# A hybrid decoder block: recurrent output transposed a step sooner and in pairs, weight casts placed behind the bank copies at every border, and the operand differences of one feed-forward block placed behind low parts

## The chip, the cores and the metric

The kernel runs on one core of a Trainium2 chip. The metric is the device time of one execution in microseconds (us); lower is better. Three runs of the kernel before are given, and one more execution was recorded by the profiler; all durations of single instructions come from that recording.

A core has a matrix engine (PE, with its weight loader PEld), a vector engine (DVE), an activation engine (ACT), a general engine (POOL) and an engine that here only issues transfers (SP). Each runs its own instructions in its own order, and they wait for one another by semaphores.

## The reference

One decoder layer over 512 positions of width 2048, in float32. Its input projection feeds eight attention heads and eight heads of a gated linear recurrence; their outputs are joined for one output projection, and a squared-ReLU network follows.

```python
h = rms_norm(x, norm1_w) * (1 + scale1) + shift1
aq, ak, av, gq, gf, gi, gg = split(h @ w_in)              # 2048 x 7168
attn = rms_norm(dilated_attention(norm_rope(aq), norm_rope(ak), av))
hg = rms_norm(hgrn2(gq, gf, gi, lb)) * silu(gg)           # 8 heads of 128
x = x + gate1 * (concat(attn, hg) @ w_out)                # 2048 x 2048
h2 = rms_norm(x, norm2_w) * (1 + scale2) + shift2
x = x + gate2 * (square(relu(h2 @ w_ff1)) @ w_ff2)        # 2048 x 8192, 8192 x 2048
```

`shift`, `scale` and `gate` are six rows that a matrix-vector product makes from the condition `c`.

## The kernel before

**Number format.** Every large product is made of three matmuls of a reduced float32 format: both operands are split into a high part (a cast on ACT) and a low part (source minus high part, on DVE). For weights this is `_split` (the cast is L39, the subtraction L40), for the activations `split_to` (L246 and L247). A matmul reads a 128x128 stationary tile and a 128x512 moving one and adds to one of eight banks; three matmuls (L205 to L207) belong to each pair of tiles.

**Input projection.** `project` (L375) computes 512 output columns in 16 steps of k, 128 rows of the weight each, with twelve matmuls a step into four banks of the tag `mm`. Its weights come in pairs of steps through `load_w` (L191): one transfer, two casts, two subtractions, with four buffers each. After the last step the four banks are copied out on ACT (`evac` L414, `hgrn_q` L572, `hg_gate` L716), and the next projection writes the same four banks; this place is called a border below. `load_w` can place its two casts behind a bank copy (`cast_behind`, used for the second pair of a projection, `k0 == 2`): the copy is kept in the list `evacuated`, which in this version only `hg_gate` fills. So the placement acts at two borders, ahead of the second gate projection and ahead of the output projection.

**Background work.** Attention, recurrence and output steps are generators in the list `tasks`; `tick` runs one step of the first of them after each step of k, so the code between two `yield`s lands between two steps of a projection. PE keeps exactly the order in which the code issues its instructions (a manual schedule from the first value projection on). ACT, DVE, POOL and SP are ordered by a scheduler ahead of the run, by priority and estimated readiness; `tc.issue_after(x)` forces an instruction to stand behind x, and `high_priority` lets it stand earlier.

**Recurrent output.** `hg_out` (L725) normalises each head's output and multiplies it by its gate (four DVE instructions of 128x128 a head, L731), and in the next step `to_mix` (L552) transposes it with four matmuls against the identity (L555) and copies the result on ACT into a tile `mix` (L557). `split_mix` splits that tile (L246, L247) into the left operand of the output projection. `korder` puts the four recurrent heads of the first group first, then eight attention heads, then the second recurrent group. The gate projection of the second group (`hg_gate(1)`) is the last ahead of the output projection, `project_out(0)`, whose first steps therefore need heads 0 to 3 of the first recurrent group, one a step. There two ticks follow each of the first ten steps.

**Feed-forward.** Both products use a seven-product scheme: per block of 1024 columns, seven products (order 1, 5, 6, 7, 3, 4, 2) of 48 matmuls (L1200 to L1202), each with four weight tiles of 128x1024. Products 5, 6, 7 and 4 need a difference of two weight tiles, made on DVE in place (`sum_of`, L1168), then the cast (L1184, ACT) and the low part (L1185, DVE). In the first feed-forward product each difference is tied behind a recent low part (`tie`); in the second product (stage 2, blocks (q, c)) it is not, and the scheduler may place several in a row.

Of the kernel before, what the change touches and what calls it, by code (L numbers as in the profile page):

```python
# [22 lines left out]
DH = 128  # L23
# [21 lines left out]
def hybrid_block(ctx, tc, x, c, positions, norm1_w, w_ada, b_ada, w_in, q_norm_w, k_norm_w,  # L45
# [3 lines left out]
    pe, dve, act, pool = nc.tensor, nc.vector, nc.scalar, nc.gpsimd  # L49
# [18 lines left out]
    def bank(name, tag="bg"):  # L68
        return ps.tile([P, 512], F32, name=name, tag=tag)
# [30 lines left out]
    n2c, aoc, hgc, posc = cols[:, 0:16], cols[:, 16:24], cols[:, 40:41], cols[:, 44:48]  # L100
# [88 lines left out]
    evacuated = []  # L189
# [45 lines left out]
    def slot(name, dt=F32):  # L235
        return io.tile([P, 512], dt, name=name, tag="io")
# [44 lines left out]
    for q in range(4):  # L281
# [5 lines left out]
        for j in range(4):  # L287
# [3 lines left out]
            t = slot("xnT")  # L291
# [117 lines left out]
    def evac(banks, name):  # L409
        ts = []  # L410
        for ti in range(NT):
            t = slot(name)
            with tc.high_priority():
                act.copy(t, banks[ti])  # L414
            ts.append(t)
        return ts

# [134 lines left out]
    def to_mix(k, src, hs, wcol):  # L552
        pt = bank("ptm")
        for ti in range(NT):
            pe.transpose(pt[:, ti * P:(ti + 1) * P], src[ti][:, hs], ident)  # L555
        mix[k] = slot("mix")
        act.activation(mix[k], pt, AF.Identity, scale=wcol)  # L557
# [8 lines left out]
    def hgrn_q(ht):  # L566
        qb = project(3072 + ht * 512, ch_mm)
        qs = []
        for h in range(4):
            q = slot("gq")  # L570
            with tc.high_priority():
                act.copy(q, qb[h])  # L572
            qs.append(q)
        for q in qs:
            sg = wk.tile([P, 512], F32, name="sg", tag="ev", bufs=2)
            act.activation(sg, q, AF.Tanh, scale=0.5)
            dve.tensor_scalar(sg, sg, 0.5 * QS, 0.5 * QS, op0=ALU.mult, op1=ALU.add)
            dve.tensor_tensor(q, q, sg, op=ALU.mult)
        return qs
# [143 lines left out]
        return gs  # L723

    def hg_out(ht, gs, os_, rs):  # L725
        for _ in range(3):
            yield
        for h in range(4):
            hs = slice(h * DH, (h + 1) * DH)
            for ti in range(NT):  # L730
                dve.scalar_tensor_tensor(gs[ti][:, hs], os_[h][:, ti * P:(ti + 1) * P], rs[:, h, ti:ti + 1],  # L731
                                         gs[ti][:, hs], op0=ALU.mult, op1=ALU.mult)
            yield
            to_mix(8 + ht * 4 + h, gs, hs, hgc)

    for b in range(4):
        bgw.append(shift_gen(b))
# [49 lines left out]
    with tc.issue_after(mod_cols.last.ins):  # L787
# [32 lines left out]
        for e in (20, 10, 0):  # L820
            u = float(2.0 ** e)
# [20 lines left out]
        for i in range(2):  # L842
            for j, (tab, h) in enumerate(((cosT, 0), (sinT, 1), (cosT, 1), (sinT, 0))):
                w = rw[:, i:i + 1, h * 16:(h + 1) * 16].broadcast_to([P, NT, 16])
# [27 lines left out]
    gs = hg_gate(0)  # L872
# [3 lines left out]
    gs = hg_gate(1)  # L876
# [27 lines left out]
    banks = project_out(0, 0, nothing)  # L904
# [52 lines left out]
    for q in range(4):  # L957
        xin = []
        for ti in range(NT):
            t = xr.tile([P, 512], F32, name="xin", tag="x")  # L960
            act.dma_start(t, x_t[:, ti, q * 512:(q + 1) * 512])
            xin.append(t)
        if q:
            banks = project_out(q, 1.7, u_split if q == 3 else nothing)
# [200 lines left out]
    def sum_of(dst, a, b, first, tie):  # L1165

        with tc.issue_after(split_done[7 if first else -2].ins) if first or tie else ExitStack():
            dve.tensor_tensor(dst, a, b, op=ALU.subtract)  # L1168

    def part(i, u, w, first, tie):  # L1170

        b11, b12, b21, b22 = (w[u, e, n] for e in range(2) for n in range(2))
        if i == 5:
            sum_of(b11, b12, b11, first, tie)
        if i == 6:
            sum_of(b11, b22, b11, first, tie)
        if i == 7:
            sum_of(b12, b22, b12, first, tie)
        if i == 4:
            sum_of(b11, b11, b21, first, tie)  # L1180
        src = {1: b11, 5: b11, 6: b11, 4: b11, 7: b12, 2: b21, 3: b22}[i]
        hi = pools[f"spl{u}"].tile([P, 2, 512], F32R, name="vhi")
        lo = pools[f"spl{u}"].tile([P, 2, 512], F32R, name="vlo")
        cast_done.append(act.copy(hi, src))  # L1184
        split_done.append(dve.tensor_tensor(lo, src, hi.bitcast(F32), op=ALU.subtract))  # L1185
        return hi, lo
# [72 lines left out]
    def turned(*a):  # L1259
        tasks.append(turn(*a))  # L1260
        while len(tasks) > 1:
            tick()
        tick()
# [59 lines left out]
    def part_of(item):  # L1323

        stage_, blk, j, i = item
        if j == 0:
            part_of.w = weights(ff1_s, 0, blk * 1024, order_of(item)) if stage_ == 1 else \
                weights(ff2_s, blk[1] * KG, blk[0] * 1024, order)
        w, first = part_of.w, blk == PLAIN // 2

        def call(u):
            with tc.high_priority() if first and j < 2 else ExitStack():
                return part(i, u, w, first, stage_ == 1)
        return call

    def order_of(item):
# [9 lines left out]
    for item, following in zip(items, items[1:] + [None]):  # L1346
        stage_, blk, j, i = item
        first = blk == PLAIN // 2
# [12 lines left out]
        if stage_ == 1:  # L1361
            banks, ahead = product(i, hparts, 0, ws, "bg" if first and j < 2 else "mm", False, call)
# [10 lines left out]
        else:  # L1373
            q, c = blk
            banks, ahead = product(i, fparts, c, ws, "mm", i == 2 and c == NC - 1, call)
# [68 lines left out]
```

## Time and profile before

| what | value |
|---|---|
| three runs | 2265.33, 2263.37, 2268.85 us; median 2265.33 |
| the profiled execution's own time | 2268.35 us |
| its span, first to last instruction | 2266.6 us (1.75 us of its time lie outside) |
| its mean granted PE clock | 0.996 |
| DVE, ACT, POOL busy | 80%, 48%, 19% |
| transfers | 598.30 MB, 264 GB/s in the mean |

A row of the timeline reads: start, duration, engine, line, operation, output and inputs, count, and in brackets how long the engine had been idle and what ended it. Rows of the list of waits read: who waited, for whom, total us, times, longest. PE's durations overlap: a matmul of 0.39 us starts 0.23 us after the one ahead of it, so its pace is read from starts.

Every matmul that this kernel needs is in its stream in both versions; PE is busy nearly all of the time, so what counts is where it is not, or where it runs at a lower clock.

### The profile page before, as it was taken

Reading aid. Unit: us, or ns where it says so; the run is one execution under the profiler, and the core shown is the slowest. Engines: PE = TensorE matmul, PEld = TensorE weight load, DVE = VectorE, ACT = ScalarE, POOL = GpSimd, SP = SyncE. Lnnn points to the kernel's source line nnn. Section 1 sums busy time; section 2 is a strip of 40 time slices with the busy share of each in tenths; the row PEclk is TensorE's granted clock in tenths of the full one; section 3 lists DMA queues with packets and bytes.
Section 4 is the critical chain, followed back from the end, with each engine's and each line's share of the span. In section 5 each row is a group of like instructions: output and inputs, shape, how many; then the busy total and the mean of one; then the engine's idle time right before and its main releaser. Section 6 shows DMA issues by size and latency. Waiting matters only on the chain.

```text
span 2266.6 us, 33052 instructions
## 1 busy us (share of the span) xinstructions
PE 2211.3 (98%) x11769; PEld 1827.6 (81%) x11769; DVE 1807.2 (80%) x2765; ACT 1098.2 (48%) x1950; POOL 439.5 (19%) x664
## 2 busy tenths in 40 slices
PE   4899999999999999999999999999999999999999
PEld 3788888888888778888887888888888888888887
DVE  6998988678977457778658988988897779967878
ACT  5555444434444454457544565565564333443332
POOL 1000022001210000003232323332232222222221
PEclk9999999999999999999999999999999999999999
DMA  9797655556564248847879789889979987998884
GB/s 327 252 330 260 214 178 167 178 177 205 174 204 145 76 134 280 273 121 263 324 278 350 285 311 387 302 302 364 336 284 372 364 313 260 349 347 312 300 298 166
DMA packets 262581, 598.30 MB, mean 264 GB/s; under 512 B 23220, under 2 KB 43968, under 8 KB 262416
## 3 DMA queue, kind: packets, MB, share of 16 engines
q1 hardware_dynamic: 186800, 332.54, 43.0%
q0 software_dynamic: 70720, 254.21, 30.6%
q10 hardware_dynamic: 4896, 9.44, 1.3%
q8 instruction: 93, 1.52, 0.3%
q14 instruction: 72, 0.59, 0.1%
HBM read 518.49 MB, written 77.61 MB: 263 GB/s over the span
## 4 chain that ended last, share of the span: by engine, by line
PE 73%; issue 10%; DMA 7%; DVE 5%; POOL 3%; ACT 1%; SPq 0%; POOLq 0%; DVEq 0%; ACTq 0%
PE f L1202 9%; PE f L1200 9%; PE f L1201 9%; PE prj L205 9%; PE prj L207 9%; PE prj L206 9%; PE f L215 2%; PE f L213 2%; PE f L214 2%; DMA Fl<-f_lod 2%; PE prj L214 2%; PE prj L215 2%; PE prj L213 2%; DMA Fl<-h_lod 1%; POOL Fl L1146 1%
## 5 line engine op out<-in xcount | busy, mean ns | idle before, releaser
L1184 ACT CAST vhi<-raw 128x1024 fp32r<-128x1024 f32 x392 | 413.3, 1055 | 520.2 <-PE f L1202 418.4
L1185 DVE TENSOR_TENSOR vlo<-raw,vhi 128x1024 fp32r<-128x1024 f32 x392 | 474.6, 1218 | 140.9 <-ACT vhi L1184 140.5
L1202 PE MATMUL f<-vhi,Fl 128*128 128x512 f32 x1376 | 535.6, 389 | 0.8 <-DMA Fl<-f_lod 0.8
L1201 PE MATMUL f<-vlo,Fh 128*128 128x512 f32 x1376 | 535.8, 389 | 0.5 <-DVE vlo L1185 0.4
L1200 PE MATMUL f<-vhi,Fh 128*128 128x512 f32 x1376 | 536.0, 390 | 0.0
L39 ACT CAST whi<-wraw 128x512 fp32r<-128x512 f32 (+1 forms) x368 | 220.4, 602 | 448.1 <-PE prj L207 297.4
L40 DVE TENSOR_TENSOR wlo<-wraw,whi 128x512 fp32r<-128x512 f32 (+1 forms) x368 | 244.2, 666 | 181.1 <-ACT whi L39 171.0
L205 PE MATMUL prj<-whi,hi 128*128 128x512 f32 x896 | 360.4, 402 | 6.4 <-ACT hi L246 5.8
L207 PE MATMUL prj<-whi,lo 128*128 128x512 f32 x896 | 351.1, 392 | 2.0 <-DVE lo L247 2.0
L206 PE MATMUL prj<-wlo,hi 128*128 128x512 f32 x896 | 350.1, 391 | 0.0
L1201 PEld LDWEIGHTS f<-vlo,Fh 128*128 128x128 f32 x1376 | 258.3, 188 | 55.3 <-DVE vlo L1185 2.0
L1202 PEld LDWEIGHTS f<-vhi,Fl 128*128 128x128 f32 x1376 | 258.3, 188 | 54.9 <-DMA Fl<-f_lod 1.2
L1200 PEld LDWEIGHTS f<-vhi,Fh 128*128 128x128 f32 x1376 | 258.3, 188 | 53.5
L1168 DVE TENSOR_TENSOR raw<-raw,raw 128x1024 f32<-128x1024 f32 x224 | 269.6, 1216 | 4.6 <-DMA raw<-in_w_ff_dram 4.2
L132 DVE SCALAR_TENSOR_TENSOR acc<-araw,sc,acc 128x512 f32<-128x512 f32 (+1 forms) x392 | 250.2, 672 | 24.6 <-DMA araw<-in_w_ada_dram 24.0
L205 PEld LDWEIGHTS prj<-whi,hi 128*128 128x128 f32 x896 | 168.8, 188 | 41.3 <-ACT hi L246 6.3
L207 PEld LDWEIGHTS prj<-whi,lo 128*128 128x128 f32 x896 | 168.8, 188 | 39.2 <-DVE lo L247 2.9
L206 PEld LDWEIGHTS prj<-wlo,hi 128*128 128x128 f32 x896 | 169.1, 189 | 32.9
L1146 POOL DMA_DIRECT2D Fh<-f_hid x112 | 79.0, 705 | 425.8 <-PE f L1202 411.0
L215 PE MATMUL f<-hi,wlo 128*128 128x512 f32 x256 | 99.9, 390 | 1.6 <-DVE wlo L40 1.6
L213 PE MATMUL f<-hi,whi 128*128 128x512 f32 x256 | 100.3, 392 | 0.0
L214 PE MATMUL f<-lo,whi 128*128 128x512 f32 x256 | 99.6, 389 | 0.0
(311 smaller groups left out, 2905.1 us busy)
## 6 DMA issues: line engine op xcount, KB each, us to landing
raw<-in_w_ff_dram SPq DMA_DIRECT2D x224, 512.0 KB, 10.5
araw<-in_w_ada_dram SPq DMA_DIRECT2D x384, 256.0 KB, 4.7
Fh<-f_hid POOLq DMA_DIRECT2D x112, 512.0 KB, 6.5
Fl<-f_lod POOLq DMA_DIRECT2D x112, 512.0 KB, 7.8
wraw<-in_w_in_dram SPq DMA_DIRECT2D x104, 512.0 KB, 4.8
Fh<-h_hid POOLq DMA_DIRECT2D x60, 512.0 KB, 6.5
Fl<-h_lod POOLq DMA_DIRECT2D x60, 512.0 KB, 6.9
f_hid<-part POOLq DMA_DIRECT2D x48, 512.0 KB, 7.6
```

Source lines behind the costliest of these rows:

```text
L39: nc.scalar.copy(hi, src)
L40: _split.low = (eng or nc.vector).tensor_tensor(lo, src, hi.bitcast(F32), op=ALU.subtract)
L132: dve.scalar_tensor_tensor(acc, raw[:, k - k0], vec[:, k:k + 1], acc, op0=ALU.mult, op1=ALU.add)
L205: pe.matmul(banks[ti], lhsT=hi[:, ts], rhs=whi, start=first, stop=False)
L206: pe.matmul(banks[ti], lhsT=hi[:, ts], rhs=wlo, start=False, stop=False)
L207: pe.matmul(banks[ti], lhsT=lo[:, ts], rhs=whi, start=False, stop=last)
L1168: dve.tensor_tensor(dst, a, b, op=ALU.subtract)
L1184: cast_done.append(act.copy(hi, src))
L1185: split_done.append(dve.tensor_tensor(lo, src, hi.bitcast(F32), op=ALU.subtract))
L1200: pe.matmul(banks[t], lhsT=fh[u][a][:, ts], rhs=whi[:, a], start=first, stop=False)
L1201: pe.matmul(banks[t], lhsT=fh[u][a][:, ts], rhs=wlo[:, a], start=False, stop=False)
L1202: pe.matmul(banks[t], lhsT=fl[u][a][:, ts], rhs=whi[:, a], start=False, stop=end)
```

## The change

Three parts:

- `evac` and `hgrn_q` now also record their last bank copy in `evacuated`, so the two casts of a projection's second pair stand behind the copies at all borders.
- `hg_out` of the first group begins one step sooner (two leading `yield`s, not three), normalises heads 0 and 1 in one step and transposes both in the next, with heads 2 and 3 following one a step. For the second group it keeps three leading steps and one head a step.
- In the first block of the second feed-forward product (`blk == (0, 0)`) the differences are tied behind low parts, as in the first product.

```diff
@@ evac
             with tc.high_priority():
-                act.copy(t, banks[ti])
+                evacuated[:] = [act.copy(t, banks[ti])]
@@ hgrn_q
             with tc.high_priority():
-                act.copy(q, qb[h])
+                evacuated[:] = [act.copy(q, qb[h])]
@@ hg_out
     def hg_out(ht, gs, os_, rs):
-        for _ in range(3):
-            yield
-        for h in range(4):
+        def normed(h):
             hs = slice(h * DH, (h + 1) * DH)
             for ti in range(NT):
                 dve.scalar_tensor_tensor(gs[ti][:, hs], os_[h][:, ti * P:(ti + 1) * P], rs[:, h, ti:ti + 1],
                                          gs[ti][:, hs], op0=ALU.mult, op1=ALU.mult)
+
+        def turned(h):
+            to_mix(8 + ht * 4 + h, gs, slice(h * DH, (h + 1) * DH), hgc)
+
+        for _ in range(2 + ht):
             yield
-            to_mix(8 + ht * 4 + h, gs, hs, hgc)
+        if ht == 0:
+            for n_, t_ in (((0, 1), ()), ((2,), (0, 1)), ((3,), ())):
+                for h in t_:
+                    turned(h)
+                for h in n_:
+                    normed(h)
+                yield
+            turned(2)
+            yield
+            turned(3)
+        else:
+            for h in range(4):
+                normed(h)
+                yield
+                turned(h)
@@ part_of
-                return part(i, u, w, first, stage_ == 1)
+                return part(i, u, w, first, stage_ == 1 or blk == (0, 0))
```

What this does to the order is shown at three places.

PE, where the second gate projection ends and the output projection begins, before. `hi_1193` belongs to the gate projection's last step of k, `hi_8713` and `hi_8789` are the output projection's first two left operands; of the twelve matmuls of each step the first stands here.

```order
L205 MATMUL prj<-whi,hi_1193 128x512
...
L555 MATMUL ptm<-ident,gg 128x128 x4
L205 MATMUL prj<-whi,hi_8713 128x512
...
L555 MATMUL ptm<-ident,gg 128x128 x8
L205 MATMUL prj<-whi,hi_8789 128x512
```

The same place after the change, where the first two left operands are named `hi_8712` and `hi_8732`:

```order
L555 MATMUL ptm<-ident,gg 128x128 x8
L205 MATMUL prj<-whi,hi_1193 128x512
...
L205 MATMUL prj<-whi,hi_8712 128x512
...
L555 MATMUL ptm<-ident,gg 128x128 x8
L555 MATMUL ptm<-ident,aq 128x128 x4
L205 MATMUL prj<-whi,hi_8732 128x512
```

Before, four transposes stood directly ahead of the step that needs their result, and the second head's directly ahead of its own step. Now both heads' stand twelve matmuls ahead of the first such step, and heads 2 and 3 are transposed a step ahead of use.

ACT at the same place, before: copies of transposes into `mix` (L557), bank copies of the gate projection (L716), weight casts (L39), casts of left operands (L246) and the gate's tanh (L720).

```order
L557 ACTIVATE mix<-ptm,cols 128x512
L716 COPY gg<-prj 128x512 x4
L39 CAST whi<-wraw 128x512 x2
L246 CAST hi_8713<-mix 128x512
L720 ACTIVATE sg<-gg 128x512 x4
L39 CAST whi<-wraw 128x512
L557 ACTIVATE mix<-ptm,cols 128x512 x2
L246 CAST hi_8789<-mix 128x512
```

And after the change:

```order
L557 ACTIVATE mix<-ptm,cols 128x512 x2
L246 CAST hi_8712<-mix 128x512
L716 COPY gg<-prj 128x512
L246 CAST hi_8732<-mix 128x512
L716 COPY gg<-prj 128x512
L720 ACTIVATE sg<-gg 128x512
L716 COPY gg<-prj 128x512 x2
L39 CAST whi<-wraw 128x512 x2
L720 ACTIVATE sg<-gg 128x512 x2
L39 CAST whi<-wraw 128x512
L557 ACTIVATE mix<-ptm,cols 128x512 x3
L246 CAST hi_8807<-mix 128x512
```

The cast of the first left operand stood behind four bank copies and two weight casts; it now stands ahead of all of them, and the second operand's cast stands behind one bank copy. A tanh now stands between the second and the third bank copy.

DVE in the first block of the second feed-forward product, before: differences (`raw<-raw,raw`) and low parts (`vlo`).

```order
L1168 TENSOR_TENSOR raw_16051<-raw_16059,raw_16051 128x1024
L1185 TENSOR_TENSOR vlo<-raw_16049,vhi 128x1024
L1168 TENSOR_TENSOR raw_16053<-raw_16061,raw_16053 128x1024
L1168 TENSOR_TENSOR raw_16055<-raw_16063,raw_16055 128x1024
L1168 TENSOR_TENSOR raw_16059<-raw_16067,raw_16059 128x1024
L1185 TENSOR_TENSOR vlo<-raw_16051,vhi 128x1024
```

And after the change:

```order
L1185 TENSOR_TENSOR raw_16051<-raw_16059,raw_16051 128x1024
L1202 TENSOR_TENSOR vlo<-raw_16049,vhi 128x1024
L1185 TENSOR_TENSOR raw_16053<-raw_16061,raw_16053 128x1024
L1202 TENSOR_TENSOR vlo<-raw_16051,vhi 128x1024
L1185 TENSOR_TENSOR raw_16055<-raw_16063,raw_16055 128x1024
L1202 TENSOR_TENSOR vlo<-raw_16053,vhi 128x1024
```

Three differences in a row between two low parts became one. (Line numbers of the changed kernel are 17 higher from `hg_out`'s end on, so its L1185 and L1202 are the L1168 and L1185 of before.)

At the nine other borders the first cast of a projection's second pair moved on ACT from ahead of the bank copies to behind them, where the second cast already stood; nothing moved on PE there.

## The prediction

> **What bounds the kernel now.** First the page's heads and the list of what PE waited for: is PE the bound, and where is it held up?
>
> ```profile
> span 2266.6 us, 33052 instructions
> PE 2211.3 (98%) x11769; PEld 1827.6 (81%) x11769; DVE 1807.2 (80%) x2765; ACT 1098.2 (48%) x1950; POOL 439.5 (19%) x664
> PE   4899999999999999999999999999999999999999
> PE prj L205 <- ACT hi L246: 5.8, 2, 4.3
> PE prj L207 <- DVE lo L247: 2.0, 2, 1.9
> PE f L1202 <- DMA Fl<-f_lod: 0.8, 1, 0.8
> PE prj L205 <- ACT aq L414: 0.5, 1, 0.5
> ```
>
> PE is busy for 2211.3 of 2266.6 us, so 55.3 us are idle. The row of digits is PE's busy share, in tenths, of 40 slices of 57 us: only the first two are below 9, and with 4 and 8 tenths they hold some 40 us of the idle time; the change leaves that start alone. The two rows on L246 and L247, 7.8 us together, are waits for the split left operand of the output projection. They are the largest that the change can reach. So second, PE's own timeline at that place:
>
> ```profile
> 786.78 0.60 PE L555 MATMUL ptm<-ident,gg 128*128 128x128 f32 x4
> 791.66 0.50 PE L205 MATMUL prj<-whi,hi 128*128 128x512 f32 x1 [4.27 <-ACT hi L246]
> 793.84 0.63 PE L207 MATMUL prj<-whi,lo 128*128 128x512 f32 x1
> 794.27 0.63 PE L205 MATMUL prj<-whi,hi 128*128 128x512 f32 x1
> 796.53 1.04 PE L555 MATMUL ptm<-ident,gg 128*128 128x128 f32 x8
> 799.08 0.50 PE L205 MATMUL prj<-whi,hi 128*128 128x512 f32 x1 [1.51 <-ACT hi L246]
> 801.70 0.50 PE L207 MATMUL prj<-whi,lo 128*128 128x512 f32 x1 [1.89 <-DVE lo L247]
> 806.95 0.47 PE L205 MATMUL prj<-whi,hi 128*128 128x512 f32 x1
> 809.80 1.03 PE L555 MATMUL ptm<-ident,aq 128*128 128x128 f32 x8
> 810.59 0.48 PE L205 MATMUL prj<-whi,hi 128*128 128x512 f32 x1
> 791.60:796.50 4.90, 4.68 (x12) 0.65 0.35 109
> 801.70:807.00 5.30, 5.30 (x23) 0.68 0.19 71
> 807.00:820.00 13.00, 13.00 (x72) 1.00 0.26 81
> ```
>
> The last three rows are stretches: us, PE's busy time and count, granted clock, transfers. From 806.95 on all runs smoothly: a step of twelve matmuls and eight transposes takes 810.59 - 806.95 = 3.64 us, of which the transposes are 810.59 - 809.80 = 0.79, so a matmul is 2.85 / 12 = 0.24 us with the start of a step in it, and 0.23 inside one. From 786.78 to 806.95 PE did 24 matmuls and 24 transposes, which are worth 2 x 3.64 + 0.79 = 8.1 us, in 20.2 us: **12.1 us were lost**. The named waits of that stretch are 4.27 + 1.51 + 1.89 and one of 0.16 us, 7.8 in all. The other 4.3 us are pace: after the waits, matmuls start 0.43 us apart (793.84 to 794.27), and the clock granted is 0.65 and 0.68.
>
> Why the first wait lasts 4.27 us shows in ACT's and DVE's timelines:
>
> ```profile
> 787.42 0.69 ACT L557 ACTIVATE mix<-ptm,cols 128x512 f32<-128x512 f32 x1 [5.26 <-PE ptm L555]
> 788.01 2.04 ACT L716 COPY gg<-prj 128x512 f32<-128x512 f32 x4
> 789.91 1.18 ACT L39 CAST whi<-wraw 128x512 fp32r<-128x512 f32 x2
> 790.95 0.66 ACT L246 CAST hi<-mix 128x512 fp32r<-128x512 f32 x1
> 791.47 1.19 ACT L720 ACTIVATE sg<-gg 128x512 f32<-128x512 f32 x2
> 797.26 1.26 ACT L557 ACTIVATE mix<-ptm,cols 128x512 f32<-128x512 f32 x2
> 798.41 1.14 ACT L246 CAST hi<-mix 128x512 fp32r<-128x512 f32 x2
> 791.81 0.69 DVE L247 TENSOR_TENSOR lo<-mix,hi 128x512 fp32r<-128x512 f32 x1
> 793.08 1.28 DVE L722 TENSOR_TENSOR gg<-gg,sg 128x512 f32<-128x512 f32 x2
> 794.29 1.65 DVE L731 SCALAR_TENSOR_TENSOR gg<-f,hrs,gg 128x128 f32<-128x128 f32 x6
> ```
>
> ACT had been idle for 5.26 us; then the transposed tile, four bank copies and two weight casts stood ahead of the one cast that PE needed. DVE made the next low parts late because it was gating and normalising the second group.
>
> **Part 1, the earlier transposes.** I walk the order after the change with these prices: a tile copy 1.15 / 2 = 0.58 us (797.26 to 798.41), a bank copy 1.90 / 4 = 0.48, a weight cast 0.52, an operand cast 0.52, a tanh 0.53 as the cast; on DVE a low part 0.61, a gate product 0.61, a normalisation 0.26, a result readable some 0.1 us after the next one starts. The gate projection's last step begins at 786.78 - 12 x 0.23 = 784.0. Now eight transposes stand there, so that step runs from 784.8 to 787.6. ACT, idle, copies the two tiles from 784.7, casts head 0 by 786.5, copies bank 0 by 786.9, casts head 1 by 787.5, then bank 1 by 787.9, one tanh, bank 2 by 788.95 and bank 3 by 789.4. The output projection's first step reuses these banks; PE wants them at 787.6, 788.3, 789.0 and 789.6, and the low part of head 0 is ready at 787.2: no wait, with 0.05 to 0.7 us to spare. The first step ends at 790.3, twelve transposes at 791.5, the second step (head 1, long ready) at 794.2, eight transposes at 795.0. ACT meanwhile does two weight casts (790.4), two tanh (791.4), a weight cast (791.95), three tile copies (793.7) and head 2's cast (794.3). DVE's queue ahead of head 2's low part is the long one: two short gate instructions, a weight low part at 793.0, two gate products to 794.25, four normalisations to 795.3, then the low part, ready at 796.0. PE's third matmul of that step wants it at 795.45: **0.6 us of wait remain**. The gain is 12.1 - 0.6 = **11.5 us**; I keep 12.1 and 7 (the first rival) as ends. The eight normalisations of heads 0 and 1 cost nothing: they were done long before, ahead of 786.78, since PE's first transposes there show no wait. The second group's heads move too, by at most a step, far ahead of their use as the last four operands. No transfer is added; on SP a group of four `w_ada` loads moves behind one more `w_out` load, and ACT's casts there waited for PE, not for loads, so this costs nothing.
>
> Does a wait of 0.6 us bring the clock down? The nearest row is one of 1.09 us in the first feed-forward product:
>
> ```profile
> 1028.34 0.50 PE L215 MATMUL f<-hi,wlo 128*128 128x512 f32 x1 [1.09 <-DVE wlo L40]
> 1028.67 0.39 PE L213 MATMUL f<-hi,whi 128*128 128x512 f32 x1
> 1028.90 0.40 PE L214 MATMUL f<-lo,whi 128*128 128x512 f32 x1
> ```
>
> Starts 0.23 us apart follow it: no loss of clock, so I charge the wait alone. The second slow stretch, 0.68 from 801.70 on, came after waits of 1.51 and 1.89 us with under 0.8 us of matmuls between them. [...]
>
> **Part 2, casts behind the copies.** It adds no instruction; at each new border it moves the first cast of the pair from ahead of the bank copies to the place where the second already stood. The rows of the tightest kind of border, where squares for the norm lie between the copies:
>
> ```profile
> 341.13 0.58 ACT L414 COPY ak<-prj 128x512 f32<-128x512 f32 x1
> 341.59 0.63 ACT L39 CAST whi<-wraw 128x512 fp32r<-128x512 f32 x1
> 343.08 0.81 DVE L40 TENSOR_TENSOR wlo<-wraw,whi 128x512 fp32r<-128x512 f32 x1
> 346.08 0.51 PE L205 MATMUL prj<-whi,hi 128*128 128x512 f32 x1
> ```
>
> The last copy is followed by the pair's second cast at 341.59; the first now stands there and the second 0.52 us behind it, and PE reads the pair's first at 346.08. With its low part at 343.08, where the second's was, it is there by 343.9: over 2 us of cover. What queues behind the moved cast on ACT (squares, small sums) is 0.52 us later, and PE waits for none of it here. The one border that cost anything, 0.5 us on a copy of `aq`, keeps its copies and squares in the same order. So nothing either way; bounds 0.5 gained and 1 lost.
>
> **Part 3, one difference at a time.** The rows of that block:
>
> ```profile
> 1662.37 2.35 DVE L1168 TENSOR_TENSOR raw<-raw,raw 128x1024 f32<-128x1024 f32 x2
> 1664.64 1.21 DVE L1185 TENSOR_TENSOR vlo<-raw,vhi 128x1024 fp32r<-128x1024 f32 x1
> 1665.91 0.50 PE L1201 MATMUL f<-vlo,Fh 128*128 128x512 f32 x1 [0.38 <-DVE vlo L1185]
> ```
>
> Two differences stood ahead of a low part that PE needed: 0.38 us of wait. The loss of pace around it is of the same size, so I take 0.7 us gained; bounds 1 gained and 1 lost. What could be late next is a difference, now just ahead of its cast: 1.14 us of DVE, 1.06 of ACT, 1.14 of DVE against a PE time of 12 x 0.23 = 2.8 us per weight tile, but tile by tile DVE needs only 2.3, and the casts run a tile ahead. The 0.8 us wait on `Fl` a little later stays: its loads start when PE frees the buffers.
>
> **Sum.** 2266.6 - 11.5 - 0.7 = 2254.4 of span, 2256.2 with the 1.75 us around it. The profiled execution took 2268.35, 3.0 more than the median of the runs, so the median to expect is **2253** us.
>
> **The rivals.**
> 1. *A wait takes the place of the one removed.* The operands of heads 2 and 3 come as late as head 1's did, since DVE still has gating and sixteen normalisations in that stretch. For it: the walk ends with just that wait, and one tanh more ahead on ACT moves it by 0.5. Then 1.51 + 1.89 and a slow stretch of 5.3 x (1 - 0.68) = 1.7 stay: the gain is 7.0 + 0.7, giving 2257.6. Against: the order puts two heads' splits ahead of these.
> 2. *The gain is given back later.* If transfers, not PE, set the pace of the feed-forward part, an earlier arrival waits there: 0.7 remains, 2264.6. Against: PE waits there for a transfer once, 0.8 us, and loads are issued as PE frees buffers, so they move along.
> 3. *The transposes are not early in effect*, because the heads are not ready: no gain at the border, 2265. Against: the first transposes of before waited for nothing.
> 4. *Slower: part 2 makes PE wait at its nine new borders.* Past the cover of about 2 us, each us of lateness of the pair costs 9 us over the borders, more with the clock. The change turns slower when each border waits over 12.2 / 9 = 1.4 us, so when the casts come about 3.5 us later than before; at 2.2 us of wait each it gives 2253 + 20 = 2273. Against: the border ahead of the second gate projection has had this placement already, and no wait stands there.
>
> **How the numbers follow.** Forecast 0.74, rival 1 0.12, rival 2 0.06, rival 3 0.04, rival 4 0.04. About 0.3%, 6.8 us, is what a measurement of this kernel can tell from no change, so faster means below 2258.5. Of the forecast 0.72 and of rival 1 0.08 lie there: faster 0.80, slower 0.04, the rest 0.16 the same. The range: 2253 less 1.4 for the better ends and about 3 for runs that scatter by 5.5 us, so 2249; upward through rival 1 with the same scatter and the part-2 loss, 2262. That leaves out rivals 2 to 4, 0.14, and little of the forecast.
>
> **What would show it.** Right: no wait of PE over 1 us between the gate projection's last step and the output projection's fourth, a granted clock of 1.00 there, and one short wait on a low part (L247). Part 2: PE's waits on L39 and L40 stay absent at the borders. Part 3: no wait on `vlo` in the block's first three products. Wrong: a wait on L246 or L716 in the first output step, clock below 0.9 there, or a longer wait on `Fl` later.

## The result, and the profile after

| | before | after |
|---|---|---|
| runs on one chip, five each | 2263.37 to 2268.85, median 2265.53 us | 2253.93 to 2260.19, median 2256.66 us |
| the profiled execution's own time | 2268.35 us | 2257.1 us |
| its span | 2266.6 us | 2255.2 us |

The ratio is 0.996 with a 95% interval of 0.9947 to 0.9974: 6 to 12 us faster. The forecast was 2253, with a range of 2249 to 2262.

First the head of the page of after, and its list of what PE waited for (who, for whom, total us, times, longest), without the rows of the kernel's start, which are as before:

```profile
span 2255.2 us, 33034 instructions
PE 2206.6 (98%) x11769; PEld 1825.2 (81%) x11769; DVE 1807.5 (80%) x2765; ACT 1096.4 (49%) x1950; POOL 440.5 (20%) x664
...
PE pD L673 <- DVE z L612: 2.0, 2, 1.0
PE pt L1247 <- DVE s L1266: 1.8, 1, 1.8
PE f L1218 <- DVE vlo L1202: 1.3, 1, 1.3
...
PE f L215 <- DVE wlo L40: 0.8, 2, 0.5
...
PE prj L205 <- ACT aq L414: 0.5, 1, 0.5
```

Of the waits of before, those on `hi` (L246, 5.8 us) and `lo` (L247, 2.0 us) and the one on `Fl` (0.8 us) are gone. Two are new: 2.0 us on `z` (L612), in the recurrence, and 1.3 us on `vlo`, 60 us behind the place where before waited 0.4. The 1.8 us on `s`, a sum of product results in the first feed-forward product, stood in before too (L1249 there).

The handover to the output projection after the change, PE, then ACT and DVE, then the same two stretches of before and of after (us; busy time and count of PE, PEld, DVE, ACT and POOL; granted clock; busy share of the transfer engines; GB/s):

```profile
785.45 1.04 PE L555 MATMUL ptm<-ident,gg 128*128 128x128 f32 x8
791.90 1.03 PE L555 MATMUL ptm<-ident,gg 128*128 128x128 f32 x8
786.09 1.26 ACT L557 ACTIVATE mix<-ptm,cols 128x512 f32<-128x512 f32 x2 [2.54 <-PE ptm L555]
787.24 0.62 ACT L246 CAST hi<-mix 128x512 fp32r<-128x512 f32 x1
787.75 0.60 ACT L716 COPY gg<-prj 128x512 f32<-128x512 f32 x1
788.23 0.64 ACT L246 CAST hi<-mix 128x512 fp32r<-128x512 f32 x1
796.89 0.68 DVE L247 TENSOR_TENSOR lo<-mix,hi 128x512 fp32r<-128x512 f32 x1
784.00:797.00 13.00, 8.57 (x34) 6.44 (x34) 6.40 (x17) 6.73 (x13) 0.00 (x0) 0.87 0.26 82
797.00:810.00 13.00, 9.60 (x44) 7.56 (x43) 7.43 (x18) 6.67 (x12) 0.00 (x0) 0.87 0.38 121
784.00:797.00 13.00, 13.00 (x73) 10.91 (x72) 8.66 (x21) 10.91 (x21) 0.00 (x0) 1.00 0.26 83
797.00:810.00 13.00, 12.86 (x67) 10.46 (x66) 11.63 (x24) 10.42 (x19) 0.00 (x0) 1.00 0.50 161
```

In these 26 us PE did 73 + 67 = 140 matmuls and transpositions after the change and 34 + 44 = 78 before, at a clock of 1.00 and of 0.87. The two casts of left operands (787.24 and 788.23) stand where the order had put them, and PE waits nowhere over 0.2 us. The rest of the working compares **leads**: the start of one and the same PE instruction in two recordings, subtracted. The last step of the gate projection began at 784.06 before; after the change the eight transpositions, now ahead of it, begin at 785.45. Further on, a transposition of the output projection's result (L936 of before, L953 of after):

```profile
784.06 0.39 PE L205 MATMUL prj<-whi,hi 128*128 128x512 f32 x1
860.58 0.60 PE L936 MATMUL pt<-ident,x 128*128 128x128 f32 x4
850.44 0.60 PE L953 MATMUL pt<-ident,x 128*128 128x128 f32 x4
```

The last row is after's: a lead of 860.58 - 850.44 = 10.1 us. But ahead of the handover after was 785.45 - 784.06 = 1.4 us **behind**. So the handover gained 11.5 us, and something ahead of it had cost over 2. The places, from leads followed through the whole span: start 0.9 gained (instructions unchanged there), 1.1 lost at 271 us, 1.0 lost at 579, 11.5 gained at the handover, 0.8 gained by 1028, 0.5 gained between 1650 and 1760, and 0.2 lost in small pieces; 11.4 together.

The two losses are PE's two new waits for `z`. DVE and PE at the first, before, and then after:

```profile
267.36 0.41 DVE L612 TENSOR_TENSOR z<-gq,f 128x256 f32<-128x256 f32 x1
269.15 1.17 DVE L659 TENSOR_TENSOR AT<-near,mt 32x128 f32<-32x128 f32 x4
270.94 0.71 PE L673 MATMUL pD<-z 128*128 128x128 f32 x4
...
267.59 1.41 DVE L132 SCALAR_TENSOR_TENSOR acc<-araw,sc,acc 128x512 f32<-128x512 f32 x2
268.92 0.55 DVE L564 TENSOR_SCALAR f<-f,omlb,lb 128x512 f32<-128x512 f32 x1
269.37 1.16 DVE L659 TENSOR_TENSOR AT<-near,mt 32x128 f32<-32x128 f32 x4
270.56 0.42 DVE L612 TENSOR_TENSOR z<-gq,f 128x256 f32<-128x256 f32 x1
271.14 0.68 PE L673 MATMUL pD<-z 128*128 128x128 f32 x4 [1.03 <-DVE z L612]
```

`z` of the recurrence's level 128 used to be done 3.2 us ahead of PE; now DVE adds four tiles to `AT`, scales `f` and does two sums of a matrix-vector product first, and PE waits 1.03 us. At the second, the additions stood ahead of `z` in before too, which PE found ready with nothing to spare; now one more low part of a weight (L40) stands there as well. None of these instructions was edited. The scheduler orders DVE, ahead of the run, by priority and estimated readiness; that its estimates moved with the casts on ACT is an inference, since no recording holds them; that the waits come with part 2 is shown below.

### The profile page after: what moved, and what is told of

Its sections match the earlier page's. It is cut to its first block, busy times and chain, and to the rows that moved or that the text cites. A ratio compares the mean times of both kernels' runs of the same rounds, so it can differ in the third digit from the quotient of the medians.

```text
span 2255.2 us, 33034 instructions
## 1 busy us (share of the span) xinstructions
PE 2206.6 (98%) x11769; PEld 1825.2 (81%) x11769; DVE 1807.5 (80%) x2765; ACT 1096.4 (49%) x1950; POOL 440.5 (20%) x664
## 3 DMA queue, kind: packets, MB, share of 16 engines
q8 instruction: 93, 1.52, 0.3%
## 4 chain that ended last, share of the span: by engine, by line
PE 87%; DVE 5%; DMA 4%; issue 1%; ACT 1%; SPq 0%; POOL 0%; DVEq 0%; ACTq 0%; POOLq 0%
PE f L1218 14%; PE f L1217 14%; PE f L1219 14%; PE prj L205 8%; PE prj L207 8%; PE prj L206 8%; PE f L215 2%; PE f L213 2%; PE f L214 2%; DMA raw<-in_w_ff_dram 2%; PE prj L214 2%; PE prj L213 2%; PE prj L215 2%; DMA araw<-in_w_ada_dram 1%; PE pt L1247 1%
## 5 line engine op out<-in xcount | busy, mean ns | idle before, releaser
L1202 DVE TENSOR_TENSOR vlo<-raw,vhi 128x1024 fp32r<-128x1024 f32 x392 | 476.1, 1224 | 138.4 <-ACT vhi L1201 138.0
L39 ACT CAST whi<-wraw 128x512 fp32r<-128x512 f32 (+1 forms) x368 | 219.5, 602 | 421.4 <-PE prj L207 277.6
L40 DVE TENSOR_TENSOR wlo<-wraw,whi 128x512 fp32r<-128x512 f32 (+1 forms) x368 | 246.0, 673 | 164.1 <-ACT whi L39 156.2
L1185 DVE TENSOR_TENSOR raw<-raw,raw 128x1024 f32<-128x1024 f32 x224 | 271.2, 1222 | 4.5 <-DMA raw<-in_w_ff_dram 4.1
```

Source lines behind the costliest of these rows:

```text
L39: nc.scalar.copy(hi, src)
L40: _split.low = (eng or nc.vector).tensor_tensor(lo, src, hi.bitcast(F32), op=ALU.subtract)
```

## The experiments

Twelve runs of ten kernels were made, each beside the kernel before on the same chip. Effects of 1 to 2 us are no larger than the intervals of the times, so what tells the theories apart is the recordings: which waits are there, and how PE's lead over the recording of before changes at one place.

### Each part alone

The edits are the three hunks of the diff, one at a time: `hg_out` alone (e1), `evac` and `hgrn_q` alone (e2), the tie alone (e3).

> Only the recurrent output's earlier, paired transposes (part 1). Theory: the whole gain is theirs and no other part helps them, so the wait of 4.27 us and those of 1.51 and 1.89 us at the handover are gone, one short wait on a low part stays, and the time is 11.5 us below the kernel before, a ratio of about 0.995; PE waits nowhere for z (L612), since the casts at the borders are as before, and the waits of 0.38 us on vlo and 0.8 us on Fl of the second product stay. Rival: the casts behind the copies are what frees ACT for the earlier operand; then a wait of over 1 us on L246 stays at the handover and the gain is under 9 us. Second rival: the lateness of z came from part 1 or from scatter between executions; then PE waits for z here too, 2.0 us.

> Only the casts behind the bank copies (part 2). Theory: the two waits of PE for z (L612) of the changed kernel, 1.0 us each, come with this part, because DVE now does the four additions to AT ahead of the z of level 128 at the first of them; the time is 2.0 to 2.3 us above the kernel before, a ratio of 1.001. Rival (the prediction's term): part 2 changes nothing, no wait for z, ratio 1.000 and a span within 0.5 us. The handover's waits, 7.8 us, stay in both.

> Only the tied differences in the first block of the second feed-forward product (part 3). Theory: the wait of 0.38 us on vlo near 1666 and that of 0.8 us on Fl go, and one of about 1.3 us on vlo, some 50 us later, takes their place, because the tied differences release their weight tiles later and so the next block's loads start later; the sum is within 0.5 us of the kernel before, ratio 1.000. Rival (the prediction's term): 0.7 us are gained, the Fl wait stays and no new wait on vlo comes.

| run | median us | ratio to before, 95% | lead gained at the handover | waits for `z` |
|---|---|---|---|---|
| e1, part 1 | 2256.89 | 0.9956 (0.9943 to 0.9968) | 11.46 us | none |
| e2, part 2 | 2265.9 | 0.9998 (0.9989 to 1.0007) | 2.67 us | 2.0 us |
| e3, part 3 | 2265.18 | 0.9995 (0.9987 to 1.0004) | 0.00 us | none |

The gain is part 1's, to the tenth: without any of the other edits the same place gives 11.46 us. Part 2 alone brings the two waits for `z`, each 1.1 us of lead, here the first, with `z` as late on DVE as in after:

```profile
270.37 0.42 DVE L612 TENSOR_TENSOR z<-gq,f 128x256 f32<-128x256 f32 x1
270.94 0.68 PE L673 MATMUL pD<-z 128*128 128x128 f32 x4 [1.03 <-DVE z L612]
```

Its time nevertheless is that of before, against what I expected. The list of waits of e2 has the 4.27 and 1.51 us of before at the handover, but the third is 0.6 us and not 1.9, and PE's stretches there say why: the first two rows are before's, the last two e2's.

```profile
792.80:796.20 3.40, 3.40 (x9) 0.51 0.49 154
803.00:806.40 3.40, 3.40 (x13) 0.50 0.03 11
790.20:797.00 6.80, 4.31 (x10) 0.53 0.24 78
799.00:806.40 7.40, 5.45 (x29) 1.00 0.43 142
```

Before ran twice at half clock here, for 3.4 us each. In e2 the low clock began during the first wait, where part of it cost nothing, made the first step slower, so that less was left to wait for afterwards, and did not come a second time. That saved 2.67 us by where the low stretches fell, in a region that part 1 clears anyway; in the changed kernel nothing is there to pay for part 2. This is one recording of e2. Its eleven times agree with those of before (ratio at most 1.0007, that is 1.6 us), and why the other ten do is not shown.

Part 3 alone did not do what either theory said. The wait on `Fl` of before is absent and a wait on `vlo` of 0.6 us, at 1736 us, stands in place of the 0.4 at 1666; the lead over that stretch (1650 to 1760) grows by 1.15 us. The prediction's rival number, 0.7, was nearer than mine, with a mechanism (the `Fl` wait stays) that fell.

### Is it DVE's order that makes z late?

The changed kernel, with the additions to `AT` tied behind `z` (e4; the line of `level` that keeps `z`'s instruction in `level.z` is left out here):

```diff
+        z128 = level(128)
         for r in range(4):
             rr = slice(r * 32, r * 32 + 32)
-            dve.tensor_tensor(AT[rr, 0:4, rr], near[rr], mt[rr, 1], op=ALU.add)
-        z128 = level(128)
+            with tc.issue_after(level.z.ins):
+                dve.tensor_tensor(AT[rr, 0:4, rr], near[rr], mt[rr, 1], op=ALU.add)
```

> The changed kernel with the additions to AT tied behind the z of level 128, so that DVE's order at that point is as in the kernel before; part 2 stays. Theory: it is DVE's order alone that made z late, so both waits for z go and the span is 2.0 us below the changed kernel's, about 2253, a ratio to the kernel before of 0.994. Rival: ACT or the weights' low parts make z late at these places, not the additions; then a wait of about 1 us for z stays at one or both of them and the span stays near 2255.

2255.43 us, ratio 0.9949 (0.9936 to 0.9963), span 2254.6. DVE and PE at the first place, then a row of e4's list of waits:

```profile
269.35 0.41 DVE L612 TENSOR_TENSOR z<-gq,f 128x256 f32<-128x256 f32 x1
270.01 0.71 PE L674 MATMUL pD<-z 128*128 128x128 f32 x4
PE pE L686 <- DVE z L612: 1.3, 1, 1.3
```

Both waits at `pD` are gone, so the order on DVE was the cause, and taking the additions out of it is enough to end them. But the `z` of level 256 is now done 0.7 us later than in after, PE is there sooner, and it waits 1.3 us at `pE` (L686), once. Of the 2.2 us of lead that after loses between 262 and 600 us, e4 still loses 1.8. The two sums and the scalings of `f` still stand ahead; a tie that puts back one instruction does not put back an order.

### What of part 1 is the step, the pair, ACT's order?

Three kernels from that of before. e6 keeps PE's order and ties the four bank copies of the second gate projection behind the first left operand's cast; e7 takes the earlier step without the pair; e8 the pair without the earlier step. (The line of e6 that keeps the cast in `split_to.hi` is left out here.)

```diff
# e6: hg_gate
-            with tc.high_priority():
+            with tc.high_priority(), tc.issue_after(split_to.hi.ins) if ht else ExitStack():
                 evacuated[:] = [act.copy(g, gb[ti])]
# e7: hg_out of before
-        for _ in range(3):
+        for _ in range(2 + ht):
# e8: hg_out of after
-        for _ in range(2 + ht):
+        for _ in range(3):
```

> The kernel before, with its transposes where they were, but the bank copies ahead of the output projection tied behind the cast of the first left operand, so that ACT's order there is as after the change. Theory: the place of the transposes on PE is what counts; the wait of 4.27 us becomes 1.3 to 1.7 (a copy of 0.6, a cast of 0.6 and a bank copy still lie between the transposes and the first matmul), the waits of 1.51 and 1.89 us for the second head stay, and the gain at the handover is 2.6 to 4.5 us. Rival: ACT's order alone was the cause, and then over 8 us come back.

> One step sooner, but one head a step (no pair). Theory: the wait of 4.27 us goes with the loss of clock after it; the second head's transposed tile now stands ahead of the bank copies on ACT, so PE waits about 1.2 us for the first bank copy, and the second step finds its operand ready; 9.5 to 10.5 of the 11.5 us are gained at the handover. Rival: the pair is needed; then the second head's waits of 1.51 and 1.89 us and the clock of 0.68 stay and the gain is about 6 us.

> Heads 0 and 1 paired, but at the old step. Theory: eight transposes directly ahead of the first output step; the first wait stays at 4 to 5 us with its low clock, the second head's waits of 1.51 and 1.89 us and the low clock after them go, and about 5 us are gained at the handover. Rival: the pair brings nothing without the earlier step, since the second cast still comes late on ACT; gain under 1.5 us.

| run | median us | ratio to before, 95% | lead gained at the handover |
|---|---|---|---|
| e6, cast first | 2261.07 | 0.9978 (0.9967 to 0.9988) | 4.9 us |
| e8, paired, late | 2260.84 | 0.9976 (0.9965 to 0.9986) | 6.0 us |
| e7, early, unpaired | 2256.55 | 0.996 (0.9947 to 0.9973) | 9.5 us |
| part 1 | 2256.89 | 0.9956 (0.9943 to 0.9968) | 11.5 us |

What PE waited for there, e6 (three rows), e8 (one), e7 (two):

```profile
789.15 0.58 PE L205 MATMUL prj<-whi,hi 128*128 128x512 f32 x1 [1.91 <-ACT gg L716]
796.67 0.50 PE L205 MATMUL prj<-whi,hi 128*128 128x512 f32 x1 [2.03 <-ACT hi L246]
798.24 0.51 PE L207 MATMUL prj<-whi,lo 128*128 128x512 f32 x1 [0.84 <-DVE lo L247]
...
791.69 0.79 PE L205 MATMUL prj<-whi,hi 128*128 128x512 f32 x1 [4.41 <-ACT hi L246]
...
788.87 0.50 PE L205 MATMUL prj<-whi,hi 128*128 128x512 f32 x1 [1.25 <-ACT gg L716]
797.96 0.50 PE L207 MATMUL prj<-whi,lo 128*128 128x512 f32 x1 [0.66 <-DVE lo L247]
```

Each piece removes the waits that its theory gave it. The earlier step does most: of the first wait 1.25 us is left, and it is for a bank copy, since the second head's transposed tile is now ahead of the copies on ACT. The pair takes away the second head's waits and the low clock behind them, and of the first wait nothing: of the 12.1 us lost in before e8 still loses 6.1, its wait of 4.41 and 1.7 of pace, the half of a low stretch of 3.4 (clock 0.52 from 791.2 to 794.6). Cast order alone gains 4.9, a little over the 4.5 that I allowed, not the 8 of its rival; the pair 6.0, where I had about 5. The step and the pair together are less than the sum of the two (9.5 + 6.0 against 11.5), because both remove the second head's waits (3.4 us in before, 0.7 left in e7, none in e8) and the stretch at half clock behind them (802.99 to 806.40 us in before, 0.50).

### What becomes of part 3, and of the changed kernel without part 2

Parts 1 and 3 without part 2 (e5, again as e12), the same with the tie extended (e9), and the changed kernel and part 1 once more (e10, e11). The tie of e9:

```diff
-                return part(i, u, w, first, stage_ == 1 or blk == (0, 0))
+                return part(i, u, w, first, stage_ == 1 or blk in ((0, 0), (0, 1)))
```

> Parts 1 and 3, the border casts as before. Theory: 11.5 us are gained at the handover and no z (L612) is late, so up to the end of the output projection PE is 11.5 us ahead of the kernel before; what is kept of it depends on the weight tiles of the first feed-forward block, whose transfers run at a full 1.04 of the 16 engines: if PE's wait for vlo near 1211 us is 2.0 us again, as with part 1 alone, the span is about 2257; if it was that execution's order of transfers alone, the wait is under 0.7 us and the span about 2253.5. Rival: that wait belongs to part 1's order of instructions; then it is there in this kernel every time, with over 3 us of vlo waits in the first block.

> Parts 1 and 3, and the differences of the second feed-forward product's second block, (0, 1), tied behind low parts as well. Theory: the wait on vlo near 1724 us (1.5 us with parts 1 and 3) comes from three differences in a row ahead of that low part, 3.6 us of DVE; with one ahead of it it is 2.3 us earlier, the wait goes, and the span is 1.5 us below the same kernel without this tie. Rival: the weight tiles come too late for that low part, as ACT's waits for them there, 1.9 to 3.3 us, suggest; then a wait of 0.5 us or more on vlo stays, or one moves to the products behind, and the span is the same.

> The changed kernel once more, on the chip of the runs beside it. Theory: two waits for z of 1.0 us each come again, as their cause is a fixed order; the wait on vlo near 1726 is over 0.5 us again; 2 us above parts 1 and 3 alone, at about 2256. Rival: the waits for z differ from execution to execution; then they are under 0.5 us here.

> Part 1 alone, once more. If the wait of 2.0 us on vlo near 1211 in its first recording was the order of transfers in that execution, it is gone or under 0.7 us and the span is about 2255; if it belongs to this kernel's order of instructions, 2 us or more of waits on vlo stand in the first feed-forward block again and the span is about 2258.

> Parts 1 and 3 once more, beside the changed kernel on one chip. Theory: no wait for z; 2 us below the changed kernel, at about 2254, if the first feed-forward block's transfers treat both alike. Rival: part 2 costs nothing in the whole, and both take the same time within 1 us.

| run | median us | ratio to before, 95% | span | lead gained at the handover | at 1650 to 1760 |
|---|---|---|---|---|---|
| e5, parts 1, 3 | 2253.36 | 0.9946 (0.9929 to 0.9963) | 2251.4 | 11.5 | 0.2 |
| e12, parts 1, 3 | 2254.48 | 0.9952 (0.9939 to 0.9964) | 2255.0 | 11.5 | 0.15 |
| e9, tied further | 2252.97 | 0.9943 (0.993 to 0.9955) | 2249.1 | 11.5 | 2.1 |
| e10, changed | 2256.06 | 0.9958 (0.9945 to 0.9972) | 2260.5 | 11.5 | -0.3 |
| e11, part 1 | 2256.38 | 0.9961 (0.9948 to 0.9975) | 2257.6 | 11.5 | 0.0 |

e9 to e12 ran on one chip. Three things follow.

*The waits for `z` are fixed.* e10 has them again (1.03 and 0.92 us), e5, e9, e11 and e12 do not. The times of e10 and e12, 1.6 us apart, are within each other's intervals.

*The new wait on `vlo` is a queue on DVE.* The rows of DVE in after, and then in e9, where it is gone:

```profile
1723.28 3.61 DVE L1185 TENSOR_TENSOR raw<-raw,raw 128x1024 f32<-128x1024 f32 x3
1726.81 1.22 DVE L1202 TENSOR_TENSOR vlo<-raw,vhi 128x1024 fp32r<-128x1024 f32 x1
...
1720.89 1.22 DVE L1185 TENSOR_TENSOR raw<-raw,raw 128x1024 f32<-128x1024 f32 x1
1722.03 1.22 DVE L1202 TENSOR_TENSOR vlo<-raw,vhi 128x1024 fp32r<-128x1024 f32 x1
```

The tie of the change had spread the differences of block (0, 0); three of the next block then stood in a row, and the low part behind them was late. In e9 they alternate there too, and PE waits for no `vlo` at all in the second product. In e9 ACT still waits for weight tiles just ahead, as it does in e5 (one row of each, e5 first):

```profile
1713.36 1.05 ACT L1201 CAST vhi<-raw 128x1024 fp32r<-128x1024 f32 x1 [2.85 <-DMA raw<-in_w_ff_dram]
1712.52 1.05 ACT L1201 CAST vhi<-raw 128x1024 fp32r<-128x1024 f32 x1 [2.82 <-DMA raw<-in_w_ff_dram]
```

So late tiles, which I had named as the cause in e3's expectation, were not it.

*A part of the gain is sometimes given back to transfers.* One and the same kernel, e5 and e12, has spans of 2251.4 and 2255.0, and e1 and e10 lose more: between 1170 and 1240, the first feed-forward block, PE waits 5.2 us in all in e1, 3.0 in e12 and 0.8 in e5. That is the prediction's second rival in small: from 1200 to 1300 the lead shrinks by 4.5 us in e1, 2.1 in e10 and 1.9 in e11, and by nothing in after. DVE there in e1, then in e5, and the stretch of both:

```profile
1204.88 1.23 DVE L1185 TENSOR_TENSOR raw<-raw,raw 128x1024 f32<-128x1024 f32 x1 [3.18 <-DMA raw<-in_w_ff_dram]
1210.04 1.23 DVE L1185 TENSOR_TENSOR raw<-raw,raw 128x1024 f32<-128x1024 f32 x1 [3.94 <-DMA raw<-in_w_ff_dram]
...
1203.26 1.23 DVE L1185 TENSOR_TENSOR raw<-raw,raw 128x1024 f32<-128x1024 f32 x1 [1.48 <-DMA raw<-in_w_ff_dram]
1205.46 1.23 DVE L1185 TENSOR_TENSOR raw<-raw,raw 128x1024 f32<-128x1024 f32 x1 [0.98 <-DMA raw<-in_w_ff_dram]
...
1170.00:1220.00 50.00, 47.28 (x205) 37.93 (x204) 38.42 (x37) 19.92 (x21) 13.19 (x19) 1.00 1.02 381
1170.00:1220.00 50.00, 49.92 (x220) 40.71 (x219) 44.19 (x43) 21.17 (x22) 13.19 (x19) 1.00 1.02 381
```

The transfer engines are full (1.02) and move the same 381 GB/s in both; what differs is when a weight tile lands: the second difference starts at 1205.46 in e5, at 1210.04 in e1 and at an estimated 1208.95 in e12, 2.41 us ahead of the end of PE's wait for the low part behind it (1211.36), which is that distance in e1 (1212.45) too.

DVE makes `s` behind these differences, and PE waits for it 1.8 to 2.0 us in ten of the fourteen recordings, before and after among them, and 0.6 to 1.1 in the other four (e5, e6, e7, e9). In before, after, e1, e10 and e11 half clock follows it, for 3.41 us in before (from 1236.48) and in after (from 1224.95); in e4 and e12 none does. So e5 and e9 gain 2.9 us on before in this stretch, which no part of their edits accounts for.

e11 decides for neither of its two cases: its wait near 1211 was 0.59 us, as if the 2.0 of e1 had been the transfers of one execution, but its span, 2257.6, is that of the other case. PE waited there for `vlo` in five of the nine recordings with the handover early (e1, e4, e10, e11, e12) and in none of the five with it late or half mended (before, e2, e3, e6, e8). That hints that an earlier arrival makes such waits more likely; with so few recordings it is not shown, and no run took transfers out of this stretch.

## Why the prediction was right, and where it was not

**The handover: right, in mechanism and size.** Worked out were 11.5 us, measured 11.45 to 11.53 in the eight recordings of this order (after, e1, e4, e5, e9 to e12). The walk through ACT's and DVE's queues found the one place left, head 2's low part, which it put at 0.6 us; the recordings show 0.13 to 0.16 us of idle time there, 0.3 by starts. The rival that a wait takes the place of the removed ones did not come about. e7 shows how near it was: without the pair PE waits 1.25 us for a bank copy and 0.66 for that low part.

**Part 2 at nothing: wrong, by 2.2 us, past its bound of 1 lost.** The step that failed is "So nothing either way", drawn from "It adds no instruction" and from the borders alone. The cover for that cast was weighed, and rightly: no wait on L39 or L40 stands at a border, and the 0.5 us on the copy of `aq` is as before. But on the engines that a scheduler orders, a moved cast moves others, far from it: the order of DVE was read only at the three places that the sum spoke of, not where PE waits with little to spare. That `z` came behind four additions at 271 us stood in the order that the scheduler fixes ahead of the run (after, e2 and e10 show the same), so it could have been read there. Rival 4 had the right engine waiting, for another thing and at ten times the price.

**Part 3 at 0.7 gained: the size nearly right, the reasons not.** Its first block lost its waits, 1.0 us as the bound had it. The wait on `Fl`, said to stay, is absent in all seven recordings with the tie and 0.4 to 1.25 us long in six of the seven without it (not in e1); why, no run tells. The "difference that could be late next" was weighed tile by tile inside the block; the price came in the block after it, 0.6 to 1.7 us on `vlo` wherever the tie ends with the first block. After's net is 0.5; over five recordings with this tie and part 1 it lies between 1.1 gained and 0.3 lost, so that one recording came near 0.7 is in part luck.

**The clock.** The prediction counted the low clock from 801.70 us on with the waits of 1.51 and 1.89 us ahead of it, and e6 bears out that a wait of that length can cost clock. The first row below is the stretch behind its single wait of 1.91 us, the second that behind its waits of 2.03 and 0.84 us:

```profile
789.20:792.80 3.60, 3.60 (x9) 0.53 0.00 0
796.20:800.00 3.80, 2.49 (x10) 1.00 0.00 0
```

The wait of 1.91 us was followed by half clock, the one of 2.03 was not. What goes with it can be read from the recordings. In before the low stretches inside the span start at 93.02, 792.75, 802.99 and 1236.48 us and again at 2263.90, behind the last matmul, in after at 91.73 and 1224.95: 205, 3, 127 and 301 times 3.4133 us apart in before and 332 times in after, as on a grid, and those between first and last matmul are one or two steps of it long (3.41 or 6.83 us). So I cut each recording into windows on its own grid and took PE's busy time, as the profiler counts it, in the window ahead:

| recording, wait of PE | window, us | PE busy in it, us | clock in the next |
|---|---|---|---|
| before, 1.89 at 801.70 | 799.58 to 802.99 | 1.52 | 0.50 |
| before, 1.82 on `s` at 1235.25 | 1233.07 to 1236.48 | 1.43 | 0.50 |
| e6, 1.91 at 789.15 | 786.02 to 789.43 | 1.50 | 0.50 |
| e6, 2.03 at 796.67 | 792.84 to 796.26 | 1.80 | 1.00 |
| e11, 2.01 on `s` at 1226.41 | 1223.12 to 1226.54 | 1.26 | 0.50 |
| e12, 2.01 on `s` at 1225.51 | 1221.61 to 1225.03 | 1.75 | 1.00 |

In before and after past the first 110 us, and in the rows of e6, e11 and e12, every window with PE busy for 1.43 us or less was followed by half clock, none with 1.75 us or more was, and the five between, of 1.47 to 1.54 us, went both ways. In these six rows, a wait of about 2 us was followed by half clock where it lay inside one window, and not where a border of the grid parted it (796.26 in e6, 1225.03 in e12). Of the pair of 1.51 and 1.89 us, the second alone lies in the window that was followed by half clock; behind the window of the first, 796.16 to 799.58 with PE busy for 1.91 us, the clock is 1.00. The last wait left at the handover was charged no clock in the prediction, and after has 1.00 there (797 to 810 us).

**The sum.** Forecast was a span of 2254.4 and 2255.2 came: part 2 took 2.2, and the start (0.9) and smaller waits by 1028 (0.8), which were not in the sum, gave most of it back. That the span came out within 0.8 us is in this part luck. The median came 3.7 above the forecast, mostly because I carried the profiled execution's distance from its median, 3.0 us, over to the changed kernel, whose profiled execution is only 0.4 above its own. That distance belongs to one execution and is no property of a kernel.

## What to carry to other kernels

Where a scheduler orders an engine, the price of an edit that adds no work is the change of order it sets off elsewhere: compare the whole order of the changed kernel, and look at each consumer that had little to spare. When a producer and its consumer share one engine queue with bulk work, put the whole chain a step ahead of use, rather than only raising one link of it: the step alone gave 9.5 of 11.5 us, the order on ACT alone 4.9. The version with the lowest median here is parts 1 and 3 with the tie extended to the next block and without part 2: 2252.97 us, beside 2256.06 for the changed kernel and 2265.45 for that of before on the same chip. Its interval overlaps the changed kernel's, so that it is the faster of the two is not shown.

## What the runs showed of the hardware

- Half clock came in stretches of 3.41 us or twice that, not in proportion to the wait: 3.41 us three times in before past the start (from 792.75, 802.99 and 1236.48) and once in after (from 1224.95), 6.83 us near the start of both (from 93.02 and 91.73), about 6.8 us in e2 (790.2 to 797.0 at 0.53) and none at all after e7's wait of 1.25 us (788 to 792 at 1.00). Waits of 1.9 to 2.0 us were followed by it in e6 (1.91) and not in e6 (2.03) or e1 (2.00 at 1212, with 1.00 from there to 1216). The starts of the low stretches are whole multiples of 3.4133 us apart in before and in after, and the grid does not fall at the same place of the program: its next border comes 1.23 us behind the end of the wait on `s` in before, 0.62 in after and 0.13 in e11. That fits equal waits faring unequally, but no run here moved the grid by itself.
- The transfer engines were full at the same 1.02 and 381 GB/s between 1170 and 1220 us in e1, e5 and e11, and a weight tile that DVE waits for still landed at different times: in two recordings of one kernel, e1 and e11, the first difference started at 1204.88 and 1206.82; in e5 and e12, again one kernel, the second started at 1205.46 and an estimated 1208.95. The spans of e5 and e12 differ by 3.6 us, and PE's waits in this stretch, 0.8 and 3.0 us, by 2.2 of it.
